# Exp of the last four rows one row at a time, and two loads of four rows joined into one, in a sum of reciprocals

## The chip, the cores and the metric

One core of one Trainium2 chip. The metric is the device time of one execution in microseconds; a kernel's time is the median of its runs. Beside the time I use a second measure from the traces, the **tail**: the end of the last sum on VectorE minus the moment at which the last input load has landed on the slowest of the 16 DMA engines. It leaves out how long the input took.

Names in what follows: PE is TensorE, the matmul engine; profile lines call ScalarE ACT, VectorE DVE and GpSimd POOL. SBUF is the memory into which the input is loaded, PSUM the one that PE's matmuls write. A chunk is two rows on each partition, worked on together.

## The reference

```python
# x: (32, 512, 1024) float32, all positive
def reference(x):
    return np.sum(1.0 / x, axis=-1).astype(np.float32)
```

The kernel sees x as 128 partitions of 128 rows with 1024 numbers each, 67.1 MB in all. The kernel does not divide. It combines a row's halves a and b: 1/a + 1/b = (a + b) / (ab), and 1/(ab) = Exp(-Ln(ab)), so ScalarE works on 512 numbers per row.

## The kernel before

Rows go in chunks of two, in three kinds `(rows, sums by PE, products by PE and VectorE)`:

```python
A, B, C = (2, 0, 0), (2, 2, 0), (2, 2, 1)
LOADS = [[A, B, A, B], [A, B, A, C]] * 5 + [[A, B], [A, C]] * 4 + [[A], [B], [A], [C]] * 2
```

In each chunk GpSimd multiplies the halves (in C it does only the second row; for the first, PE copies a half to PSUM (`b`) and VectorE multiplies). ScalarE makes Ln and then Exp. The row sum is one VectorE instruction: for A it multiplies the whole row (1024) with the Exp in PSUM (`rc`), for B and C it multiplies the Exp (`pr`, 512) with a + b, which PE has added into a PSUM tile (`s`).

```python
def sum_rows(c, xc, pr, sm, rc):            # VectorE, for the chunk before
    m, e = xc.shape[1], len(sm)
    for j in range(e, m):                   # kind A
        ...
        sum_row(c + j, row, rc[:, j - e, :]..., ...)
    for j in reversed(range(e)):            # kinds B and C: second row first
        sum_row(c + j, pr[:, j, :], sm[j])

...
    for (m, e, v), pr in zip(chunks, made):
        ...                                  # GpSimd products
        sm = []
        for j in range(e):                   # PE: first row first
            s = spool.tile([P, H], f32, tag="s")
            add(s, xc[:, j, :H], xc[:, j, H:])
            sm.append(s)
        if waiting:
            sum_rows(*waiting)
        keep(nc.scalar.activation(out=pr, in_=pr, func=Ln, scale=S))
        rc = None
        if e < m:
            rc = rpool.tile([P, m - e, H], f32, tag="rc")
            i = nc.scalar.activation(out=rc, in_=pr[:, e:, :], func=Exp, scale=-1.0)
            keep(i)
        if e:
            r = pr[:, :e, :]
            keep(nc.scalar.activation(out=r, in_=r, func=Exp, scale=-1.0))
        waiting = c0 + q, xc, pr, sm, rc
```

The last two chunks are an A (rows 124, 125) and a C (126, 127).

## Time and profile before

| | before |
|---|---|
| time, median of 4 runs (lowest to highest) | 171.83 us (171.72 to 171.97) |
| span of the profiled execution | 169.9 us |
| last input landed, slowest DMA engine | 161.06 us |
| last sum over | 167.14 us |
| tail | 6.08 us |

The prediction below shows the page's header and the tail's lines on ScalarE and VectorE. Read a timeline line as: start in us, duration in us, engine, line of the kernel, operation, output<-inputs, shapes, count, and in brackets the idle time before it with the instruction that ended it.

### The profile page before, as it was taken

To read this page: it belongs to the slowest core of one execution; us is meant where nothing else is said; L and a number is where in the kernel's file an instruction comes from. 1 tells how busy PE (TensorE), PEld (TensorE's weight loads), DVE (VectorE), ACT (ScalarE), POOL (GpSimd) and SP (SyncE) were. 2 spreads that over 40 slices of the span, in tenths; PEclk is the share of its full clock that TensorE was granted. 3 is DMA by queue.
4 is the path that set the end of the run, shared out by engine and by line. 5 is a ranking of instruction groups with operands and counts; after the bars stand their busy time and mean duration, and the time that the engine had idled before them with its cause. 6 is when DMAs were issued, how large, how long until landed. Compare 5 with 4: busy or idle time off the path is not lost.

```text
span 169.9 us, 1267 instructions
## 1 busy us (share of the span) xinstructions
PE 131.7 (77%) x278; PEld 50.5 (30%) x278; DVE 122.3 (72%) x267; ACT 133.9 (79%) x129; POOL 138.3 (81%) x70
## 2 busy tenths in 40 slices
PE   0008999786988789784997869789999999888790
PEld 0003433331332233231432323224334342333230
DVE  0000777767987577767777679778989898889883
ACT  3002989978887987958889787999999988999890
POOL 1008999699996999689996998999999889998920
PEclk9999999999999999999999999999999999999999
DMA  6999999999999999999999999999999999999400
GB/s 208 409 455 409 463 409 455 409 463 401 463 411 447 424 440 420 432 434 424 440 424 440 424 397 434 424 428 426 432 428 432 424 413 417 422 420 424 187 0 15
DMA packets 3894, 67.24 MB, mean 396 GB/s; under 512 B 432, under 2 KB 560, under 8 KB 560
## 3 DMA queue, kind: packets, MB, share of 16 engines
q1 hardware_dynamic: 3888, 67.18, 92.9%
q8 instruction: 2, 0.03, 0.1%
q14 instruction: 4, 0.03, 0.0%
HBM read 67.11 MB, written 0.07 MB: 395 GB/s over the span
## 4 chain that ended last, share of the span: by engine, by line
DMA 78%; POOL 11%; DVE 3%; ACT 2%; issue 2%; SPq 1%; POOLq 0%; DVEq 0%
DMA ring<-in_x_dram 78%; POOL pr L141 11%; DVE pr L92 2%; DVE ring L92 1%; ACT pr L152 1%; ACT rc L156 1%; SPq L122 1%; POOLq L141 0%; DVE sums L92 0%; DVEq L92 0%; DVEq L195 0%
## 5 line engine op out<-in xcount | busy, mean ns | idle before, releaser
L141 POOL TENSOR_TENSOR pr<-ring 128x1024 f32<-128x1024 f32 x64 | 137.6, 2189 | 23.6 <-DMA ring<-in_x_dram 23.3
L82 PE MATMUL s<-ring,ident 128*128 128x512 f32 x256 | 122.4, 616 | 32.5 <-DVE sums L92 16.6
L152 ACT ACTIVATE pr<-pr 128x1024 f32<-128x1024 f32 x64 | 67.4, 1053 | 28.7 <-POOL pr L141 28.5
L82 PEld LDWEIGHTS s<-ring,ident 128*128 128x128 f32 x256 | 47.0, 194 | 105.3 <-issue 63.1
L92 DVE CUSTOM_DVE_ANT_1 pr<-ring,rc 128x1024 f32<-128x1024 f32 x32 | 39.1, 1221 | 44.6 <-ACT rc L156 44.6
L92 DVE CUSTOM_DVE_ANT_0 pr<-pr,s 128x512 f32<-128x512 f32 x64 | 41.3, 683 | 0.2
L92 DVE CUSTOM_DVE_ANT_1 ring<-ring,rc 128x1024 f32<-128x1024 f32 x32 | 38.9, 1216 | 0.0
L162 ACT ACTIVATE pr<-pr 128x1024 f32<-128x1024 f32 x32 | 33.8, 1058 | 1.0
L156 ACT ACTIVATE rc<-pr 128x1024 f32<-128x1024 f32 x32 | 32.9, 1028 | 1.0
L82 PE MATMUL b<-ring,ident 128*128 128x512 f32 x22 | 12.0, 626 | 1.4 <-DMA ring<-in_x_dram 1.4
L92 DVE DVE_READ_ACCUMULATOR2_ANT sums<- 128x1 f32 x128 | 10.6, 83 | 0.0
L130 DVE TENSOR_TENSOR pr<-ring,b 128x512 f32<-128x512 f32 x11 | 7.5, 683 | 0.1
L82 PEld LDWEIGHTS b<-ring,ident 128*128 128x128 f32 x22 | 3.5, 188 | 9.0 <-DMA ring<-in_x_dram 7.6
L53 ACT ACT_TABLE_LOAD x1 | 1.3, 1283 | 0.7 <-PEq L184 0.7
masks.py:197 POOL MEMSET ident<- 128x128 f32 x1 | 0.2, 204 | 0.3 <-POOLq L184 0.3
masks.py:199 POOL TENSOR_SCALAR_AFFINE_SELECT ident<-ident 128x128 f32<-128x128 f32 x1 | 0.3, 292 | 0.1
L184 POOL MEMSET const-float32-0.0<- 128x1 f32 x1 | 0.1, 98 | 0.2 <-issue 0.2
L184 POOL MEMSET const-uint8-127<- 128x1 uint8 x1 | 0.1, 103 | 0.0
L184 POOL MEMSET const-bfloat16-1.0<- 128x1 bf16 x1 | 0.1, 101 | 0.0
L184 POOL MEMSET const-float32-1.0<- 128x1 f32 x1 | 0.1, 98 | 0.0
## 6 DMA issues: line engine op xcount, KB each, us to landing
ring<-in_x_dram SPq DMA_DIRECT2D x10, 4096.0 KB, 37.8
ring<-in_x_dram SPq DMA_DIRECT2D x8, 2048.0 KB, 37.0
ring<-in_x_dram SPq DMA_DIRECT2D x8, 1024.0 KB, 28.3
out_dram<-sums SPq DMA_DIRECT2D x1, 64.0 KB, 1.5
```

The lines of the kernel that those rows point to most:

```text
L53: nc.scalar.add_instruction(mybir.InstLoadActFuncSet(name=nc.get_next_instruction_name(), act_func_set_id=act_sets.index("natural_log_exp_ ...
L82: i = nc.tensor.matmul(bank, lhsT=ident, rhs=half, start=k == 0, stop=k == len(halves) - 1,)
L92: i = nc.vector.tensor_tensor_reduce(out=row if out is None else out, in0=row, in1=fac, scale=S, scalar=0.0, op0=mult, op1=plus, accum_out ...
L122: keep(nc.sync.dma_start(out=xt, in_=x_v[:, c0 : c0 + n, :]))
L130: i = nc.vector.tensor_tensor(out=pr[:, j, :], in0=xt[:, q + j, :H], in1=b, op=mult)
L141: i = nc.gpsimd.tensor_tensor(out=pr[:, v:, :], in0=xc[:, v:, :H], in1=xc[:, v:, H:], op=mult)
L152: keep(nc.scalar.activation(out=pr, in_=pr, func=Ln, scale=S))
L156: i = nc.scalar.activation(out=rc, in_=pr[:, e:, :], func=Exp, scale=-1.0)
L162: keep(nc.scalar.activation(out=r, in_=r, func=Exp, scale=-1.0))
L184: nc = _bacc.Bacc("TRN2", target_bir_lowering=False, num_devices=1)
```

## The change

The intent: let VectorE begin with row 124 when half of the Exp is done, hand over the last two rows in the same way, and save the queue one load.

```diff
+    SINGLE = 124
-    LOADS = [[A, B, A, B], [A, B, A, C]] * 5 + [[A, B], [A, C]] * 4 + [[A], [B], [A], [C]] * 2
+    LOADS = [[A, B, A, B], [A, B, A, C]] * 5 + [[A, B, A, C]]
+    LOADS += [[A, B], [A, C]] * 3 + [[A], [B], [A], [C]] * 2
...
-                pr[:, e : e + 2, :] if j == e and m - e > 1 else None,
+                pr[:, e : e + 2, :] if j == e and e + 1 < m and c < SINGLE else None,
...
-            rc = None
-            if e < m:
-                rc = rpool.tile([P, m - e, H], f32, tag="rc")
-                i = nc.scalar.activation(out=rc, in_=pr[:, e:, :], func=Exp, scale=-1.0)
-                keep(i)
-            if e:
-                r = pr[:, :e, :]
+            step = 1 if c0 + q >= SINGLE else m
+            rc = []
+            for j in range(e, m, step):
+                to = min(j + step, m)
+                r = rpool.tile([P, to - j, H], f32, tag="rc")
+                keep(nc.scalar.activation(out=r, in_=pr[:, j:to, :], func=Exp, scale=-1.0))
+                rc += [r[:, l, :] for l in range(to - j)]
+            for to in range(e, 0, -step):
+                r = pr[:, max(to - step, 0) : to, :]
                 keep(nc.scalar.activation(out=r, in_=r, func=Exp, scale=-1.0))
```

(Line breaks are joined and the matching index of `rc` in the sums is cut.) The order of PE, GpSimd and VectorE instructions is unchanged.

More of the change, by code (lines that the diff above doesn't have):

```diff
@@ L110, in sum_rows @@
                 row,
-                rc[:, j - e, :].unsqueeze(1).to_broadcast([P, 2, H]),
-                pr[:, e : e + 2, :] if j == e and m - e > 1 else None,
+                rc[j - e].unsqueeze(1).to_broadcast([P, 2, H]),
+                pr[:, e : e + 2, :] if j == e and e + 1 < m and c < SINGLE else None,
             )
@@ L152 @@
             keep(nc.scalar.activation(out=pr, in_=pr, func=Ln, scale=S))
-            rc = None
-            if e < m:
-                rc = rpool.tile([P, m - e, H], f32, tag="rc")
-                i = nc.scalar.activation(
-                    out=rc, in_=pr[:, e:, :], func=Exp, scale=-1.0
-                )
-                keep(i)
-            if e:
-                r = pr[:, :e, :]
+            step = 1 if c0 + q >= SINGLE else m
[3 more added lines that the diff above has]
+                r = rpool.tile([P, to - j, H], f32, tag="rc")
+                keep(
+                    nc.scalar.activation(
+                        out=r, in_=pr[:, j:to, :], func=Exp, scale=-1.0
+                    )
+                )
+                rc += [r[:, l, :] for l in range(to - j)]
+            for to in range(e, 0, -step):
+                r = pr[:, max(to - step, 0) : to, :]
                 keep(nc.scalar.activation(out=r, in_=r, func=Exp, scale=-1.0))
```

## The prediction

> **What bounds the kernel now.** I read the header of the page first, then the timeline of its last 18 us, then the chain of waits, then the trace's records of landings.
>
> ```profile
> span 169.9 us, 1267 instructions
> PE 131.7 (77%) x278; PEld 50.5 (30%) x278; DVE 122.3 (72%) x267; ACT 133.9 (79%) x129; POOL 138.3 (81%) x70
> ...
> DMA packets 3894, 67.24 MB, mean 396 GB/s; under 512 B 432, under 2 KB 560, under 8 KB 560
> ...
> DMA 78%; POOL 11%; DVE 3%; ACT 2%; issue 2%; SPq 1%; POOLq 0%; DVEq 0%
> ```
>
> No compute engine is over 81% of the span, and 78% of the chain that ended last is the load of the input. In the table by stage the DMA share is 0.99 to 1.02 from 10 us to 155 us. So the input stream runs without a hole. The trace's records of each load's landing say the same: the median of the 16 DMA engines advances by 9.71 us per load of eight rows (4096 KB, so 432 GB/s), 4.89 us per load of four (429 GB/s) and 2.48 us per load of two (422 GB/s). The last load lands at 158.97 us on the fastest engine and at 161.06 us on the slowest. Nothing in the kernel can end before 161.06 plus the work that hangs on the last rows. Everything up to there is the stream; the remaining 8.9 us of the 169.9 are the tail.
>
> The tail is the last two chunks of two rows: chunk A (rows 124 and 125, all products on GpSimd, both row sums on VectorE from an Exp in PSUM) and chunk C (126 and 127, one product by PE and VectorE, sums from PE). These are its lines on ScalarE and then VectorE:
>
> ```profile
> 161.17 1.06 ACT L152 ACTIVATE pr<-pr 128x1024 f32<-128x1024 f32 x1 [0.33 <-POOL pr L141]
> 162.26 1.03 ACT L156 ACTIVATE rc<-pr 128x1024 f32<-128x1024 f32 x1
> 163.23 1.04 ACT L152 ACTIVATE pr<-pr 128x1024 f32<-128x1024 f32 x1
> 164.30 1.06 ACT L162 ACTIVATE pr<-pr 128x1024 f32<-128x1024 f32 x1
> ```
>
> ```profile
> 162.26 0.69 DVE L130 TENSOR_TENSOR pr<-ring,b 128x512 f32<-128x512 f32 x1
> 163.32 1.22 DVE L92 CUSTOM_DVE_ANT_1 pr<-ring,rc 128x1024 f32<-128x1024 f32 x1 [0.37 <-ACT rc L156]
> 164.47 0.08 DVE L92 DVE_READ_ACCUMULATOR2_ANT sums<- 128x1 f32 x1
> 164.47 1.22 DVE L92 CUSTOM_DVE_ANT_1 ring<-ring,rc 128x1024 f32<-128x1024 f32 x1
> 165.61 0.08 DVE L92 DVE_READ_ACCUMULATOR2_ANT sums<- 128x1 f32 x1
> 165.84 0.69 DVE L92 CUSTOM_DVE_ANT_0 pr<-pr,s 128x512 f32<-128x512 f32 x1
> ...
> 166.45 0.68 DVE L92 CUSTOM_DVE_ANT_0 pr<-pr,s 128x512 f32<-128x512 f32 x1
> ```
>
> The reader is to see one hole: VectorE ends the product of row 126 at 162.26 + 0.69 = 162.95 and stands idle for 0.37 us until 163.32, because the Exp of rows 124 and 125 (162.26 to 163.29) is a single instruction and the first row sum needs only its first half. From 163.32 to 167.14 VectorE has four sums one behind the other, two of 1.14 us pitch and two of 0.61, with one gap of 0.15 us before 165.84. The last Exp was over at 164.30 + 1.06 = 165.36, before VectorE got to it, so after 163.32 VectorE alone sets the end. Then follow 1.5 us for the output transfer and the close.
>
> **What the Trainium skill says.** (1) "ScalarE: Activation LUTs", section "What ACT_TABLE_LOAD costs": an ACTIVATE with immediate scale and bias takes 186 ns plus 0.833 ns per element, and back-to-back ones overlap by about 93 ns. For 1024 elements that is 1039 ns; the trace has 1053 (Ln), 1058 (Exp to SBUF) and 1028 (Exp to PSUM), so it agrees within 2%. The overlap shows smaller: 163.23 against an end at 163.29, so 0.06 us. (2) "Perfetto Trace Analysis", section "Optimizing Scalar/DVE Operations": where these engines aren't saturated but cause bubbles on others, "breaking up instructions may allow work to be completed sooner". This is the intent here; the bubble is the 0.37 us. (3) "DMA: Bandwidth & Descriptors", section "Bandwidth": a table in which 1 MB takes 6.15 us (341 GB/s) and 16 MB run at 425 GB/s. That would make load size weighty. The trace disagrees for loads queued behind one another: 1 MB loads arrive every 2.48 us, so 422 GB/s, only 2.3% below the 4 MB loads.
>
> **The change part by part.**
>
> Loads. Two loads of four rows (80 to 83, 84 to 87) become one of eight. Their cost in the queue is 2 x 4.89 = 9.78 us against 9.71, so 0.07 us less on every engine. (The packet records agree in sign: a packet of 32 KB takes 1.213 us, two of 16 KB take 1.230; with eight packets per engine that is 0.14. I take 0.08.) Everything landing later, the last load included, comes about 0.08 us sooner. The kinds of chunk stay A, B, A, C, and the comparison of instruction orders shows the same order on every engine. The other side is that rows 80 to 83 now arrive with 84 to 87, at about 111.8 us instead of 106.95. GpSimd finishes rows 72 to 79 at 102.54 + 8.27 = 110.8, so it idles about 1.1 us that it did not idle before. It gets this back: in the kernel before it waits 0.94 us at 136.45 and 0.23 us at 141.37 for data, together 1.17, and 0.60 more at 153.80. The delay is gone before the tail. The issue of the bigger load needs rows 40 to 47 consumed, at some 73 us (its predecessor landed at 62.24, plus about 10 us of compute), while the queue holds loads up to 102 us. The stream can't run dry there.
>
> Exp in pieces. In the last two chunks two Exps of 1024 elements become four of 512. By slope and base a half takes 186 + 427 = 613 ns (estimate from page (1)), or 0.60 us in PSUM, where the trace is 11 ns under the formula. First, chunk A: row 124 is ready at 162.26 + 0.60 = 162.86, before VectorE is free at about 162.93 (elsewhere a row sum starts 0.65 us after the start of such a product: 153.50 and 154.15). Its sum therefore starts at 162.93 instead of 163.32: **0.39 us saved**. Row 125 is ready at about 163.4, needed at 164.07. The whole of both Exps is over 0.1 to 0.15 us later than before, so the Ln of chunk C moves from 163.23 to some 163.35 and ends at 164.40. Row 127 (taken first, as the sums are) is ready at 164.42 + 0.63 = 165.05, needed at about 165.3 to 165.45; row 126 at 165.6, needed at 166.0. Hence the extra 0.2 to 0.3 us on ScalarE lie beside VectorE's sums and cost nothing. The split in chunk C also gains nothing, since the unsplit Exp would end at 165.5, at most 0.15 us late.
>
> Sum in place. For row 124 the product is written into the ring instead of the tile still being read; the trace has 1221 and 1217 ns for the two forms. Zero.
>
> Sum: 0.08 + 0.39 = 0.47 us. 171.85 - 0.47 = 171.4, or 0.3% less.
>
> **The rivals.** *ScalarE becomes the end.* If halves cost clearly more than 0.61 us (0.75, say), the row sums of chunk C would wait for their Exp: row 127 at 165.35, row 126 at 166.05, still about level with VectorE. The gain would shrink to 0.3 us. Against it: page (1) agrees so well at 1024 elements. *The bigger load leaves a lasting delay.* If GpSimd or the engines behind it don't recover their 1.1 us, the gain vanishes and up to 0.6 us is added: 171.9 to 172.5. For it: the engines run at 96% to 99% between 120 and 140 us (PE 19.78, ACT 19.31, POOL 19.06 of 20). Against it: GpSimd's waits for data at 136 to 154 us are 1.77 us together. *The slowest DMA engine moves.* The 16 engines land 0.84 us apart in the first load and 2.1 us apart from 82 us on: the packet records show instruction fetches (four of 8 KB, two of 16 KB) in between, and the spread grew by about 1 us beside the 16 KB one at 66 us. The end hangs on the slowest engine. With another program the fetches could meet other engines: 1 us either way, 170.5 or 172.5. Against: the three runs lie within 0.25 us, so it is not random, and the change adds only two ACTIVATEs.
>
> **Range and chances.** Middle 171.4, with 0.3 us for the terms worked out and up to 1 us in the rarer case of the fetches, gives 170.8 to 172.0. The borders of 2% lie at 168.4 and 175.3; no rival reaches either. Chances: 0.01 faster, 0.98 same, 0.01 slower.
>
> **What would show it.** The changed trace should have: VectorE's first sum of row 124 starting right at the end of the product of row 126, without the 0.37 us idle before it; four Exps of 512 elements at 0.60 to 0.65 us; no idle time on VectorE before the sums of rows 127 and 126 above 0.2 us; the last row landing at about 161.0; GpSimd idle about 1 us near 111 us and on data again by 141 to 154 us; and the last sum ending near 166.7. A last landing later than 161.3 or a GpSimd still behind at 153 us would make the prediction wrong.

## More of the kernel before

The prediction did not use PE's part of the tail, though the timeline that was asked for beforehand has it. This is the view, the timeline of PE near the end of the kernel before:

```profile
161.10 1.13 PE L82 MATMUL b<-ring,ident 128*128 128x512 f32 x2 [1.16 <-DMA ring<-in_x_dram]
162.06 3.60 PE L82 MATMUL s<-ring,ident 128*128 128x512 f32 x8
```

PE starts when the last load lands, makes the copy for row 126's product and then the sums for rows 126 and 127, in this order, until 162.06 + 3.60 = 165.66. VectorE takes row 127 first, so its first sum of the last chunk can't start before 165.66.

## The result, and the profile after

| | before | after |
|---|---|---|
| time, median of 4 runs (lowest to highest) | 171.83 us (171.72 to 171.97) | 171.75 us (171.73 to 172.01) |
| last input landed, slowest engine | 161.06 us | 161.04 us |
| last sum over | 167.14 us | 167.10 us |
| tail | 6.08 us | 6.06 us |

The ratio of after to before is 0.9998, with a 95% interval of 0.9981 to 1.0016. The time lies in the predicted range, and the kernel is neither faster nor slower by 2%; but of the forecast gain of 0.47 us nothing is to be seen.

The page of the changed kernel, its header and the shares of the chain that ended last:

```profile
span 170.0 us, 1264 instructions
...
DMA 63%; POOL 15%; ACT 10%; issue 4%; DVE 3%; PE 3%; DVEq 0%; POOLq 0%; SPq 0%
```

PE was not in this list before, and now it is. The timeline of ScalarE and then of VectorE, the same stretch that the prediction shows of the kernel before:

```profile
161.12 1.06 ACT L154 ACTIVATE pr<-pr 128x1024 f32<-128x1024 f32 x1 [0.31 <-POOL pr L143]
162.21 1.12 ACT L162 ACTIVATE r<-pr 128x512 f32<-128x512 f32 x2
163.27 1.04 ACT L154 ACTIVATE pr<-pr 128x1024 f32<-128x1024 f32 x1
164.34 1.15 ACT L169 ACTIVATE pr<-pr 128x512 f32<-128x512 f32 x2
```

```profile
162.25 0.69 DVE L132 TENSOR_TENSOR pr<-ring,b 128x512 f32<-128x512 f32 x1
162.94 1.22 DVE L94 CUSTOM_DVE_ANT_1 ring<-ring,r 128x1024 f32<-128x1024 f32 x1
164.09 0.08 DVE L94 DVE_READ_ACCUMULATOR2_ANT sums<- 128x1 f32 x1
164.09 1.22 DVE L94 CUSTOM_DVE_ANT_1 ring<-ring,r 128x1024 f32<-128x1024 f32 x1
165.23 0.08 DVE L94 DVE_READ_ACCUMULATOR2_ANT sums<- 128x1 f32 x1
165.79 0.69 DVE L94 CUSTOM_DVE_ANT_0 pr<-pr,s 128x512 f32<-128x512 f32 x1 [0.48 <-PE s L84]
166.41 0.08 DVE L94 DVE_READ_ACCUMULATOR2_ANT sums<- 128x1 f32 x1
166.41 0.68 DVE L94 CUSTOM_DVE_ANT_0 pr<-pr,s 128x512 f32<-128x512 f32 x1
```

The first hole is closed as forecast: the sum of row 124 starts at 162.94, where it started at 163.32. A new one has opened: before the sum of row 127 VectorE waits 0.48 us for `s`, PE's sum. That sum starts at 165.79, 0.05 us before its time in the kernel before. PE's own lines in the changed kernel, and the end of the chain of waits:

```profile
161.09 1.12 PE L84 MATMUL b<-ring,ident 128*128 128x512 f32 x2 [1.17 <-DMA ring<-in_x_dram]
162.05 3.60 PE L84 MATMUL s<-ring,ident 128*128 128x512 f32 x8
```

```profile
141.21 19.84 DMA ring<-in_x_dram
161.04 0.04 issue
161.09 1.12 PE b L84 x2
162.21 3.45 PE s L84 x8
165.66 0.03 issue
```

PE ends at 165.65, as it did before. The chain now runs load, PE, VectorE and leaves ScalarE out. The question for the experiments: was PE the bound already, so that the split had nothing to give, or does something else eat the gain, such as the larger load or the halved Exps?

### The profile page after: what moved, and what is told of

It is laid out like the page before. It is cut to its first block, busy times and chain, and to the rows that moved or that the text cites. A ratio compares the mean times of both kernels' runs of the same rounds, so it can differ in the third digit from the quotient of the medians.

```text
span 170.0 us, 1264 instructions
## 1 busy us (share of the span) xinstructions
PE 131.9 (78%) x278; PEld 50.8 (30%) x278; DVE 122.5 (72%) x267; ACT 134.1 (79%) x131; POOL 138.3 (81%) x70
## 4 chain that ended last, share of the span: by engine, by line
DMA 63%; POOL 15%; ACT 10%; issue 4%; DVE 3%; PE 3%; DVEq 0%; POOLq 0%; SPq 0%
DMA ring<-in_x_dram 63%; POOL pr L143 15%; ACT pr L154 6%; PE s L84 2%; DVE ring L94 2%; ACT r L162 2%; ACT pr L169 2%; DVE pr L94 1%; PE b L84 1%; DVE pr L132 0%; DVEq L202 0%; DVE sums L94 0%; POOLq L143 0%; SPq L124 0%; DVEq L94 0%
## 5 line engine op out<-in xcount | busy, mean ns | idle before, releaser
L154 ACT ACTIVATE pr<-pr 128x1024 f32<-128x1024 f32 x64 | 67.3, 1052 | 28.6 <-POOL pr L143 28.5
L94 DVE CUSTOM_DVE_ANT_1 pr<-ring,r 128x1024 f32<-128x1024 f32 x31 | 37.9, 1221 | 43.3 <-ACT r L162 43.1
L94 DVE CUSTOM_DVE_ANT_1 ring<-ring,r 128x1024 f32<-128x1024 f32 x33 | 40.1, 1217 | 0.0
L169 ACT ACTIVATE pr<-pr 128x1024 f32<-128x1024 f32 (+1 forms) x33 | 33.9, 1031 | 1.0
L162 ACT ACTIVATE r<-pr 128x1024 f32<-128x1024 f32 (+1 forms) x33 | 33.0, 1001 | 1.0
L84 PEld LDWEIGHTS b<-ring,ident 128*128 128x128 f32 x22 | 4.0, 201 | 9.4 <-DMA ring<-in_x_dram 7.5
```

Of the source, the lines that this page charges most:

```text
L84: i = nc.tensor.matmul(bank, lhsT=ident, rhs=half, start=k == 0, stop=k == len(halves) - 1,)
L94: i = nc.vector.tensor_tensor_reduce(out=row if out is None else out, in0=row, in1=fac, scale=S, scalar=0.0, op0=mult, op1=plus, accum_out ...
L162: nc.scalar.activation(out=r, in_=pr[:, j:to, :], func=Exp, scale=-1.0)
```

## The experiments

Eight kernels ran, all with correct results. Those of the first four shared one chip and eleven runs of the kernel before (median 172.13 us, 171.76 to 172.86); the last four shared another chip, also with eleven (172.39 us, 171.65 to 172.78). The spread of 1.1 us is over four times that of the first measurement, and the traces show where it lies: the last landing of the profiled executions falls anywhere from 160.92 to 162.36 us. So the verdicts rest on the tail, and the times stand beside it.

Each tail comes from one trace. How well it repeats, e1 and e2 tell: e1 has the tail of the changed kernel (both 6.06) and e2 that of the kernel before (6.09 and 6.08). Tails can be compared because they begin alike: in the nine traces other than e8, PE's copy for row 126 starts 0.04 to 0.05 us after the last landing, and the Ln of rows 124 and 125 0.08 to 0.12 us after it.

| kernel | last landing | last sum over | tail | median us | ratio to before (95%) |
|---|---|---|---|---|---|
| before | 161.06 | 167.14 | 6.08 | 171.83 | |
| after | 161.04 | 167.10 | 6.06 | 171.75 | 0.9998 (0.9981 to 1.0016) |
| e1 split only | 161.71 | 167.77 | 6.06 | 172.37 | 1.0010 (0.9988 to 1.0033) |
| e2 loads only | 160.92 | 167.01 | 6.09 | 172.09 | 1.0004 (0.9973 to 1.0035) |
| e3 after, PE's order | 162.12 | 167.64 | 5.52 | 171.70 | 0.9968 (0.9946 to 0.9990) |
| e4 before, PE's order | 162.36 | 168.21 | 5.85 | 172.39 | 1.0018 (0.9997 to 1.0039) |
| e5 after, VectorE's order | 161.64 | 167.13 | 5.49 | 171.75, one run | |
| e6 after, PE's sum twice | 161.90 | 169.67 | 7.77 | 174.39, one run | |
| e7 as e3, only A split | 161.06 | 166.85 | 5.79 | 171.52, one run | |
| e8 tail by rows | 161.31 | 166.53 | 5.22 | 171.02 | 0.9936 (0.9909 to 0.9963) |

### e1 and e2: each part alone

e1 takes the changed kernel with the old `LOADS`; e2 takes the kernel before with the new one:

```diff
 e1, against after
-    LOADS = [[A, B, A, B], [A, B, A, C]] * 5 + [[A, B, A, C]]
-    LOADS += [[A, B], [A, C]] * 3 + [[A], [B], [A], [C]] * 2
+    LOADS = [[A, B, A, B], [A, B, A, C]] * 5 + [[A, B], [A, C]] * 4 + [[A], [B], [A], [C]] * 2
 e2, against before: the same lines the other way round
```

> The Exps of the last four rows split, the loads as in the kernel before. T1 (PE's last sum of row 127, ending at 165.66 us in both traces, holds the sums of chunk C; the 0.39 us that the split frees on VectorE turn into a wait for PE): time within 0.15 us of the kernel before, about 171.8, with VectorE's first sum of row 124 at about 162.95 and a wait of 0.4 to 0.5 us for PE before the sum of row 127. R1 (the split gains its 0.4 us and the larger load gives it back): about 171.4.

> One load of eight rows in place of two of four, the Exps whole as in the kernel before. T1: the last landing stays at about 161.05 us and the time within 0.15 us of the kernel before, about 171.8. R1 (the larger load costs what the split gains): about 172.2.

Neither moves: tails of 6.06 and 6.09 us. So the split gains nothing even without the larger load, and R1 falls. (What the larger load does to the landing, e2's times can't tell to better than 0.5 us.) In e1's timeline of VectorE the new wait stands with the old loads too:

```profile
166.47 0.69 DVE L93 CUSTOM_DVE_ANT_0 pr<-pr,s 128x512 f32<-128x512 f32 x1 [0.46 <-PE s L83]
```

e2 shows something about the kernel before as well. Its Exps are whole, its first sum of chunk A still waits 0.36 us for ScalarE, and yet there is a wait for PE:

```profile
163.18 1.22 DVE L93 CUSTOM_DVE_ANT_1 pr<-ring,rc 128x1024 f32<-128x1024 f32 x1 [0.36 <-ACT rc L157]
164.33 1.22 DVE L93 CUSTOM_DVE_ANT_1 ring<-ring,rc 128x1024 f32<-128x1024 f32 x1
...
165.71 0.69 DVE L93 CUSTOM_DVE_ANT_0 pr<-pr,s 128x512 f32<-128x512 f32 x1 [0.16 <-PE s L83]
```

### e3 and e4: PE makes row 127's sum first

The same exchange on both kernels. PE does the same work; only the sum that VectorE takes first is made first:

```diff
-            sm = []
-            for j in range(e):
+            sm = [None] * e
+            for j in reversed(range(e)) if c0 + q >= 126 else range(e):
                 s = spool.tile([P, H], f32, tag="s")
                 add(s, xc[:, j, :H], xc[:, j, H:])
-                sm.append(s)
+                sm[j] = s
```

> The changed kernel, with PE making the sum of row 127 before that of row 126 in the last chunk, as VectorE needs them in this order; the number of instructions is unchanged. T1: row 127's PE sum is over at about 163.9, row 126's at 165.66; VectorE goes from row 125 to row 127 at about 165.4 with a gap under 0.2 us and ends at 166.6 to 166.75, so 0.35 to 0.45 us less than the changed kernel: about 171.35. R2 (the wait is put down to PE but belongs to ScalarE's halved Exps or to something else): 171.75, unchanged.

> The kernel before with the same exchange on PE alone. T1: two chains end together there (VectorE's sums of rows 124 and 125 at 165.69, PE's sum at 165.66), so freeing one gains at most the gap of 0.15 us in front of row 127's sum: 171.7 to 171.85. R3 (PE alone held the end of the kernel before): about 0.4 us less, 171.4.

e3's VectorE has no wait left in the tail:

```profile
164.06 1.22 DVE L94 CUSTOM_DVE_ANT_1 ring<-ring,r 128x1024 f32<-128x1024 f32 x1
165.21 1.22 DVE L94 CUSTOM_DVE_ANT_1 ring<-ring,r 128x1024 f32<-128x1024 f32 x1
166.35 0.68 DVE L94 CUSTOM_DVE_ANT_0 pr<-pr,s 128x512 f32<-128x512 f32 x1
166.96 0.68 DVE L94 CUSTOM_DVE_ANT_0 pr<-pr,s 128x512 f32<-128x512 f32 x1
```

Its tail is 6.06 - 5.52 = 0.54 us shorter than that of the changed kernel, more than the 0.35 to 0.45 I had written down, since the gap before row 127 vanishes altogether: the four sums follow at 1.15, 1.14 and 0.61 us. The ratio of 0.9968 has its whole interval below 1. R2 falls.

e4 shows the kernel before in a new light:

```profile
164.63 1.22 DVE L92 CUSTOM_DVE_ANT_1 pr<-ring,rc 128x1024 f32<-128x1024 f32 x1 [0.37 <-ACT rc L156]
165.78 1.22 DVE L92 CUSTOM_DVE_ANT_1 ring<-ring,rc 128x1024 f32<-128x1024 f32 x1
166.92 0.68 DVE L92 CUSTOM_DVE_ANT_0 pr<-pr,s 128x512 f32<-128x512 f32 x1
```

The wait for ScalarE is untouched, but the last sums follow with no gap, and the tail is 6.08 - 5.85 = 0.23 us shorter. I had expected at most 0.15 (T1) or 0.4 (R3); neither number holds. In the kernel before, row 125's sum starts at 164.47, the next could follow at a pitch of 1.14, at 165.61, and it starts at 165.84: 0.23 late. I had read the gap as 0.15, from the end of the accumulator read to the next start, but here that read overlaps the next sum. In the five traces in which PE holds row 127 (before, after, e1, e2, e6), its sum starts 0.15 to 0.18 us after the end of PE's last matmul, so 165.66 on PE means 165.84 on VectorE. So **PE held the end of the kernel before, with VectorE's chain 0.23 us behind it**. The tails of the four combinations say the rest: the split alone is worth 0.02 us, PE's order alone 0.23, both together 0.56 (6.08 - 5.52). With PE out of the way the split is worth 5.85 - 5.52 = 0.33 us. In time e4 is not shown to be faster: its ratio is 1.0018 (0.9997 to 1.0039), and its profiled run, the slowest of the six, has the latest landing of all, 162.36 us. Its 0.23 us stand in the tail alone.

### e5: VectorE's order instead of PE's

```diff
-        for j in reversed(range(e)):
+        for j in range(e) if c >= 126 else reversed(range(e)):
             sum_row(c + j, pr[:, j, :], sm[j])
...
-            for to in range(e, 0, -step):
+            for to in range(e, 0, -step) if c0 + q < 126 else range(1, e + 1):
```

> The changed kernel, with ScalarE's halved Exps and VectorE's sums of the last chunk taken in the order 126, 127 instead of 127, 126; PE's order is left. The tail (end of the last sum minus the last landing of input) was 6.08 us before and 6.06 us in the changed kernel. T1 (VectorE waits for the PE sum that is made last): the same cure as exchanging the order on PE, tail 5.5 us, no wait over 0.1 us in front of the two sums. R2 (something in PE's order itself made the gain): tail 6.06 us.

5.49 us, as T1 says. It is the mismatch of the two orders that costs the time, not one of the orders.

### e6: the suspected cost doubled

```diff
-                add(s, xc[:, j, :H], xc[:, j, H:])
+                for _ in range(2 if c0 + q + j == 127 else 1):
+                    add(s, xc[:, j, :H], xc[:, j, H:])
```

> The changed kernel with PE's sum of row 127 made twice (4 more matmul records of 0.43 us; the result is the same). T1 (PE's last sum sets the end of the changed kernel one for one): tail 6.06 + 1.72 = 7.8 us, with a wait for PE of about 2.2 us before the sum of row 127. R2 (PE isn't what the end waits for): part of the 1.72 us is hidden, tail under 7.4 us.

PE's line grows from 3.60 to 5.31 us, the wait on VectorE from 0.48 to 2.16 us, and the tail by 7.77 - 6.06 = 1.71 us: one for one.

```profile
162.91 5.31 PE L84 MATMUL s<-ring,ident 128*128 128x512 f32 x12
```

```profile
168.37 0.69 DVE L94 CUSTOM_DVE_ANT_0 pr<-pr,s 128x512 f32<-128x512 f32 x1 [2.16 <-PE s L84]
```

### e7: only chunk A split

```diff
 against e3
-            step = 1 if c0 + q >= SINGLE else m
+            step = 1 if SINGLE <= c0 + q < 126 else m
```

> Only the Exp of rows 124 and 125 is split, that of 126 and 127 is whole, and PE has the exchanged order. T1 with ScalarE hidden: the whole Exp ends about 3.3 + 1.06 us after the last landing, 0.1 to 0.15 us after VectorE is through with row 125; tail 5.55 to 5.7 us, against 5.52 with both split. R4 (both splits are needed for the gain): tail 5.85 us or more, as without any split.

5.79 us, between the two expectations. These are its lines of ScalarE and VectorE:

```profile
164.36 1.06 ACT L169 ACTIVATE pr<-pr 128x1024 f32<-128x1024 f32 x1
```

```profile
165.55 0.69 DVE L94 CUSTOM_DVE_ANT_0 pr<-pr,s 128x512 f32<-128x512 f32 x1 [0.21 <-issue]
```

The whole Exp is over at 165.42, and VectorE starts row 127 at 165.55, while row 125's sum at 164.11 would have let it start at 165.25. The view does not name the releaser ("issue"), but e7 differs from e3 in this one Exp alone. The split of the last chunk is worth 5.79 - 5.52 = 0.27 us once PE is away; I had put it at nothing. The split of chunk A, to which the prediction gave the whole 0.39 us, is worth 5.85 - 5.79 = 0.06 us without it: once chunk A is split and PE is away, ScalarE's whole Exp of the last chunk holds the end. (The last chunk's split without chunk A's was not run.)

### e8: the tail row by row

Here GpSimd's products and Ln are cut to rows as well, and the last chunk becomes a B, so that PE makes no copy before its sums:

```diff
-    LOADS += [[A, B], [A, C]] * 3 + [[A], [B], [A], [C]] * 2
+    LOADS += [[A, B], [A, C]] * 3 + [[A], [B], [A], [C], [A], [B], [A], [B]]
...
+            step = 1 if c0 + q >= SINGLE else m
+            for j in range(v, m, step):                # GpSimd's product, row by row
...
+                if step < m:                           # Ln just ahead of each row's Exp
+                    keep(nc.scalar.activation(out=r, in_=r, func=Ln, scale=S))
```

(with e5's order of the sums)

> A version meant to beat both kernels: in the last two chunks GpSimd's products, Ln, Exp and sums go row by row, the last chunk has all products on GpSimd (so PE begins its sums at once, 1.1 us sooner), and VectorE takes row 126 before 127. T1 (the tail is a chain of whole chunks through GpSimd, ScalarE, PE and VectorE, and shrinks as each hands on sooner): row 124's sum can start right after that of row 122, about 1.1 us after the last landing instead of 1.9, tail about 4.9 us, so 1.1 us less than the kernel before, about 0.6%. R5 (finer instructions cost what they free: GpSimd's two half products or ScalarE's eight halves take over): tail 5.5 us or more.

The tail is 5.22 us, in between: 0.86 us less than before, where I had hoped for 1.1. The time is 171.02 us against 172.39, a ratio of 0.9936, below 1 with its whole interval. The changed kernel was not run beside it; its tail is 0.84 us longer than e8's. e8 changes several things at once, so no run says which of them brings how much. What ends the gain is R5's ScalarE. From 160.99 to 165.81 it goes without a hole through eight half-size instructions, and VectorE waits for the last:

```profile
164.53 0.61 ACT L174 ACTIVATE pr<-pr 128x512 f32<-128x512 f32 x1
165.18 0.63 ACT L175 ACTIVATE pr<-pr 128x512 f32<-128x512 f32 x1
```

```profile
165.84 0.69 DVE L94 CUSTOM_DVE_ANT_0 pr<-pr,s 128x512 f32<-128x512 f32 x1 [0.44 <-ACT pr L175]
```

## Why the prediction was right or wrong

**The bound up to the tail: right.** The stream runs to 161.04 us and nothing before it matters. GpSimd's new wait near 112 us (forecast about 1.1 us) is 1.11 us; after it comes a stretch without waits, and at 153.75 it waits 0.63 us for data, as before the change (0.60 at 153.80). The delay of the larger load is gone by then, as said:

```profile
111.91 41.22 POOL L143 TENSOR_TENSOR pr<-ring 128x1024 f32<-128x1024 f32 x20 [1.11 <-DMA ring<-in_x_dram]
153.75 7.33 POOL L143 TENSOR_TENSOR pr<-ring 128x1024 f32<-128x1024 f32 x3 [0.63 <-DMA ring<-in_x_dram]
```

**The loads' 0.08 us: not confirmed.** In the two traces every landing after the joined load is 0.06 to 0.11 us earlier up to 141.13 (141.24 before), but the last one only 0.02. Where the rest went I can't say: an instruction fetch of 16 KB stands at 140.75 us in the changed kernel and at 134.96 in the one before, but no run tells whether it is the cause. Landings differ by over 1 us between executions, so a term of this size isn't to be settled with eight runs.

**Halved Exps: right in their cost.** Two in a row take 1.12 us in PSUM and 1.15 in SBUF, singly 0.60 and 0.63 in e8. "ScalarE: Activation LUTs" of the Trainium skill, section "What ACT_TABLE_LOAD costs", gives by its formula, as an estimate, 2 x 613 - 93 = 1133 ns for the pair. Row 124's sum starts at 162.94, forecast 162.93. Measured from the last landing, it starts 1.90 to 1.94 us later in the six traces (e8 apart) with chunk A's Exp split, and 2.26 to 2.27 in the three without, so the 0.39 us are really 0.32 to 0.37. The Ln of the last chunk moves by 0.04 us, forecast 0.12.

**The step that failed** is the sentence "so after 163.32 VectorE alone sets the end". It was drawn from ScalarE's and VectorE's lines alone. PE's last sum, at 165.66, held the end already, and the 0.38 us by which row 124's sum came earlier turned into a 0.48 us wait for PE. e3, e5 and e6 show this from three sides and e4 that it was so before the change. The clue was in sight: a "gap of 0.15 us before 165.84" with no named cause. It was really 0.23 us, and its cause was PE. The forecast "no idle time on VectorE before the sums of rows 127 and 126 above 0.2 us" was the check that failed. Among the rivals a second producer for the same sum was missing: the list had ScalarE, the load and the DMA engines, but the sum of row 127 reads two tiles, `pr` and `s`.

**"The split in chunk C also gains nothing":** right in the kernel as changed, as it lies behind PE; wrong as a statement on ScalarE. With PE away the split of chunk A, credited with all, brings 0.06 us alone, and that of the last chunk the other 0.27 (e7). So "VectorE alone" had overlooked ScalarE as well.

**The range held by luck,** as far as the mechanism goes: its width came from instruction fetches on the DMA engines, for which up to 1 us was allowed, and the missing 0.47 us fits inside. On one point the prediction was too sure: "it is not random". On the two chips of the experiments the same kernel varies by 1.1 us from run to run.

**Slips that changed nothing.** From the end of the last sum to the end of the span it is 169.9 - 167.14 = 2.8 us, not 1.5. GpSimd's 19.06 of 20 us are 95%, not 96%. The overlap of 0.06 us between two ACTIVATEs is that after an Exp into PSUM; after one into SBUF it is 0.09 us (an end at 156.43, the next start at 156.33).

## What to carry to other kernels

An instruction that reads two tiles has two chains in front of it, and shortening one is worth only its lead over the other: list the producers of every operand and their end times before counting a gain. The page "Perfetto Trace Analysis" of the Trainium skill, section "Identifying Dependency Chains", says to look at the semaphores that an instruction waits for; in the trace of the kernel before, the sum of row 127 waits for semaphores of PE (last raised at 165.67), ScalarE (165.36) and GpSimd (162.51), and that would have shown the second chain. A producer should make first what its consumer takes first; matching the two orders cost no instruction and was worth more than the change itself.

## What the Trainium skill lacked or had wrong

- "Perfetto Trace Analysis", section "Optimizing Scalar/DVE Operations", says that breaking up instructions may let work finish sooner. It lacks the condition: with another producer ending as late, the 0.38 us freed turned into a 0.48 us wait and the tail went from 6.08 to 6.06 us; with that producer reordered, the same split was worth 0.33 us.
- "DMA: Bandwidth & Descriptors", section "Bandwidth", gives 341 GB/s for a transfer of 1 MB, in a table of transfers issued from GpSimd. It lacks a figure for loads queued behind one another: here, issued from SyncE, loads of this size arrived every 2.48 us, which is 422 GB/s, and 4 MB loads at 432 GB/s.
- None of the pages tells of packets that slow down in groups. In e3's packet records eight packets of 32 KB that start from 46.1 to 47.1 us took 2.12 to 2.47 us instead of 1.213. The traces of before, after and e7 have no such group behind the start, and their last landings are 161.04 to 161.06 us; the other seven have groups, and six of them land later, up to 162.36 us (e2, with a group near 56 us, lands at 160.92). So this is most likely what moves the landing, though no run tests it; what makes the groups is open.
